# Feed-forward of a streaming encoder layer: two scheduled passes made one product with a written order, and two normalisation factors moved behind the down product

## The chip, the cores and the metric

The kernel runs on one core of one Trainium2 chip. A core has TensorE (PE, matrix products into PSUM, with PEld for its weight loads), VectorE (DVE), ScalarE (ACT), GpSimd (POOL) and SyncE (SP), whose queue issues the transfers. Each engine works off its own queue in order and waits at semaphores for the others. The metric is the device time of one execution in microseconds; the time before is 1810.67 us, the median of three runs (1808.79 to 1811.64).

## The reference

One inference step of a one-layer encoder over 1152 tokens (1024 of a prompt and eight streams of 16): attention beside a gated convolution, cross-attention into a memory, and a gated feed-forward with a causal convolution. Only the last part is touched:

```python
x = x + xo.reshape(b, t_len, D_MODEL) @ w_xo
hf = rms_norm(x, g_ffn)
u_c, new_ffn = causal_dwconv(hf @ w_up, ffn_state, w_ffconv)
x = x + (jax.nn.silu(u_c) * (hf @ w_gate)) @ w_down
...
y_prompt = rms_norm(hp, g_final)
```

The model width is 1024 and the hidden width 2816, that is 8 and 22 blocks of 128. All is float32, and each product of two float32 matrices is made of three passes: both operands are split into a high part and the rest (`h`, `l`), and h·h, h·l and l·h are summed in PSUM. The norm's factor r of a token scales a whole column here (tokens lie along the free axis), so it may be multiplied in before or after a product.

## The kernel before

**Layout.** Activations stand transposed: 128 features in the partitions, 1152 tokens along the free axis. A *split* (`split`, L111 and L112) is a copy on ACT that rounds to the high part (`wh`, `t`, `gx`) and a subtraction on DVE or POOL that gives the rest (`wl`).

**Output projection of the cross-attention** (`residual_wino`). Eight output blocks, each over three token chunks of 384, 24 matmuls a chunk (L148 to L150). When a chunk leaves PSUM, DVE adds the residual (L985, tile `xc`), the sum goes to memory, DVE multiplies by the gain (L987, into `xg`), and ACT and POOL add up the squares. The operand pieces `b` of the next product are split as they come. After the last block stands the norm: a reciprocal over all 1152 tokens (L1005), products with a matrix of ones that sum the squares (L1009), and `rstd` (L190 to L195), whose result is multiplied into the tile `r`.

**Up and gate** (`ffn_up`, `wino`). Two blocks of 128 hidden features at a time form a 2x2 block product in Strassen-Winograd form: seven products P1 to P7 in place of eight, on sums of weights (S1 to S4, POOL, L1030 to L1033) and differences of activations (T1 to T4). A *product* here is 24 matmuls of 288 tokens (L1051). P1 and P2 accumulate in PSUM chain a, P6, P7 and P4 in chain b, P5 and P3 in chain c; between them ACT (L1065, L1072) and DVE (L1061) read the chains into the output tiles `u` (up) or `g` (gate). One call for `u` and one for `g` make a *pair* of 14 products, and there are 11 pairs. In `ffn_conv` (between the two calls) POOL multiplies `u` by r (L1088), ACT and DVE run the three-tap convolution (L1100 to L1104) and ACT the silu (L1105); POOL multiplies its result by r a second time (L1106), for the gate's half, which has not had its r. DVE multiplies with `g` (L1138), and the product goes to the scratch `gscr`.

**Down** (`ffn_down`). For token blocks of 512, 384 and 256 and eight output blocks j: 22 k-tiles times 3 matmuls. The hidden operands are loaded from `gscr` and split into `gx` while j is 0, the weights are loaded and split again for each token block, with the rests on DVE and POOL in turn. `norm` applies the last normalisation, one block late.

**What sets the order.** A scheduler orders each engine's instructions by priorities and modelled times, and places a transfer, a wait or a product of the next stage where it finds room; buffers are counted per pool (three PSUM chains `ch`, three weight buffers, two raw ones).

Of the kernel before, what the change touches and what calls it, by code (L numbers as in the profile page):

```python
# [11 lines left out]
F32R = mybir.dt.float32r  # L12
AF = mybir.ActivationFunctionType
# [38 lines left out]
class Step:  # L52
# [42 lines left out]
    def sm(self, cols):  # L95

        return self.tile("small", "t8", [8], 32)[:, 0:cols]

    def bank(self, tag):
        return self.tile("psum", tag, [1024 if tag in ("sc", "ch") else 512], 3 if tag == "ch" else 2)  # L100
# [868 lines left out]
    def residual_wino(self, wsrc, xh, xl, xsrc, dst, gi):  # L969
# [3 lines left out]
        xg = [None] * KT  # L973
        acc = self.tile(self.tp, "acc", [T])
        self.B = [{} for _ in range(4)]
        self.Tf = [None] * 4
        for n in range(KT):
            j = n // 2 + 4 * (n % 2)
            xg[j] = self.tile("xg", "xg", [T], KT)

            def evac(c, ps):
                cs = slice(c * CH, (c + 1) * CH)
                x = self.tile(self.tp, "xc", [CH], 3)
# [3 lines left out]
                nc.vector.scalar_tensor_tensor(out=xg[j][:, cs], in0=x, scalar=self.g[:, gi, j:j + 1], in1=self.r[:, cs],  # L987
                                               op0=ALU.mult, op1=ALU.mult)
                self.sumsq(acc[:, cs], x, n == 0, sq=self.tile(self.tp, "sq", [CH], 2))

            self.block(wsrc[j], xh, xl, lambda c: ("mm", "tr")[(c + n) % 2], evac)
            if n % 2 == 0:
                k = n // 2
                self.B[k]["B11"] = self.pair("hl", "b", xg[j][:, 0:HT])
            else:
                a, b = xg[j - 4], xg[j]
                b11, b12, b21, b22 = a[:, 0:HT], a[:, HT:T], b[:, 0:HT], b[:, HT:T]
                self.B[k]["B21"] = self.pair("hl", "b", b21)
                self.B[k]["B22"] = self.pair("hl", "b", b22)
                nc.vector.tensor_tensor(out=b11, in0=b12, in1=b11, op=ALU.subtract)  # L1000
                nc.vector.tensor_tensor(out=b12, in0=b22, in1=b12, op=ALU.subtract)
                nc.vector.tensor_tensor(out=b22, in0=b22, in1=b11, op=ALU.subtract)
                nc.vector.tensor_tensor(out=b21, in0=b21, in1=b22, op=ALU.subtract)
                self.Tf[k] = {"T1": b11, "T2": b22, "T3": b12, "T4": b21}
        nc.vector.reciprocal(out=self.r, in_=self.r)  # L1005
        for c in range(NCH):
            cs = slice(c * CH, (c + 1) * CH)
            ps = self.bank("sc")[:, :CH]
            nc.tensor.matmul(ps, lhsT=self.ones, rhs=acc[:, cs], start=True, stop=True)  # L1009
            y, v = (self.tile(self.tp, "xc", [CH], 3) for _ in range(2))  # L1010
            r = self.tile(self.tp, "sq", [CH], 2)
            self.rstd(r, ps, 1.0 / D, CH, y, v)
            nc.vector.tensor_tensor(out=self.r[:, cs], in0=self.r[:, cs], in1=r, op=ALU.mult)
# [6 lines left out]
    def wino_raw(self, u0, u1):  # L1020
        return self.wraw(u0), self.wraw(u1)

    def wino(self, raws, dst, first=False):

        nc = self.nc
        a11, a12 = raws[0][:, 0:512], raws[0][:, 512:1024]
        a21, a22 = raws[1][:, 0:512], raws[1][:, 512:1024]
        s3, s2, s4 = (self.tile("ws", "S", [512], 3) for _ in range(3))
        tt = nc.gpsimd.tensor_tensor
        tt(out=s3, in0=a11, in1=a21, op=ALU.subtract)  # L1030
        tt(out=a21, in0=a21, in1=a22, op=ALU.add)
        tt(out=s2, in0=a21, in1=a11, op=ALU.subtract)
        tt(out=s4, in0=a12, in1=s2, op=ALU.subtract)  # L1033
        opd = {"P1": (a11, "B11"), "P2": (a12, "B21"), "P3": (s4, "B22"), "P4": (a22, "T4"),
               "P5": (a21, "T1"), "P6": (s2, "T2"), "P7": (s3, "T3")}
        ch = {}

        def product(p, c, start):
            x, b = opd[p]
            h, l = self.tile("weights", "wh", [512], 3, F32R), self.tile("weights", "wl", [512], 3, F32R)  # L1040
            self.split(h, l, x)
# [12 lines left out]
        def bank(c):  # L1054
            return ch[c].rearrange("p (t n) -> p t n", t=2)[:, :, 0:HC]

        def sb(m, t):
            return dst[m][t].rearrange("p (t n) -> p t n", t=2)

        def add(m, t, c, y):  # L1060
            nc.vector.tensor_tensor(out=sb(m, t), in0=bank(c), in1=sb(*y), op=ALU.add)  # L1061

        p1 = 1, 0
        product("P1", "a", True)
        nc.scalar.copy(out=sb(*p1), in_=bank("a"))  # L1065
        if first:
            product("P2", "a", False)
        product("P6", "b", True)
        if not first:
            product("P2", "a", False)  # L1070
        add(0, 1, "b", p1)
        nc.scalar.copy(out=sb(0, 0), in_=bank("a"))  # L1072
        product("P7", "b", False)
        product("P5", "c", True)
        add(1, 1, "b", p1)
        product("P4", "b", False)
        add(1, 1, "c", (1, 1))
        product("P3", "c", False)
        add(1, 0, "b", p1)
        add(0, 1, "c", (0, 1))  # L1080


    def ffn_conv(self, f, u):

        nc, I = self.nc, self.I
        st = self.tile("tu", "sff", [NB, 2], 2)
        nc.sync.dma_start(out=st, in_=I["sff"][f])
        nc.gpsimd.tensor_tensor(out=u[:, HALO:HALO + T], in0=u[:, HALO:HALO + T], in1=self.r, op=ALU.mult)  # L1088
        v = self.tile("tu", "vs", [NB, HALO + TS], 2)
        us = u[:, HALO + S_P:HALO + T].rearrange("p (b t) -> p b t", t=TS)  # L1090
        nc.gpsimd.tensor_copy(out=v[:, :, 0:HALO], in_=st)
        nc.gpsimd.tensor_copy(out=v[:, :, HALO:], in_=us)
        new = self.tile("tu", "nff", [18], 2)
        nc.gpsimd.tensor_copy(out=new[:, 0:2], in_=u[:, S_P:S_P + HALO])
        nc.gpsimd.tensor_copy(out=new[:, 2:18].rearrange("p (b t) -> p b t", t=2), in_=v[:, :, TS:TS + 2])
        nc.sync.dma_start(out=self.O["nff"][f], in_=new)
        s = self.tile("tu", "s", [T], 2)
        w = self.wff[:, f]
        sp, ss = s[:, 0:S_P], s[:, S_P:T].rearrange("p (b t) -> p b t", t=TS)
        nc.scalar.activation(sp, u[:, 0:S_P], AF.Identity, scale=w[:, 0:1])  # L1100
        nc.scalar.activation(ss, v[:, :, 0:TS], AF.Identity, scale=w[:, 0:1])
        for j in (1, 2):
            for o, x in ((sp, u[:, j:j + S_P]), (ss, v[:, :, j:j + TS])):
                nc.vector.scalar_tensor_tensor(out=o, in0=x, scalar=w[:, j:j + 1], in1=o, op0=ALU.mult, op1=ALU.add)  # L1104
        nc.scalar.activation(s, s, AF.Silu)  # L1105
        nc.gpsimd.tensor_tensor(out=s, in0=s, in1=self.r, op=ALU.mult)  # L1106
        return s

    def ffn_up(self):

        nc, I = self.nc, self.I

        def halves(z, o=0):
            return z[:, o:o + HT], z[:, o + HT:o + T]
# [303 lines left out]
```

## Time and profile before

| | |
|---|---|
| time, median of three runs | 1810.67 us |
| profiled execution, own time | 1811.96 us |
| profiled execution, span from first to last instruction | 1810.2 us |
| start of the output projection of the cross-attention | about 799 us |
| its last matmul | about 899 us |
| first product of up and gate starts | 916.0 us |
| first matmul of down starts | 1486.5 us |
| last matmul of down ends | about 1798.6 us |

The span is cut at these points because the change reaches only what lies behind 799 us. Times inside the trace are microseconds from the span's start. A row of the timeline or of the chain of waits begins with start and duration; a row of a table of stretches gives the stretch, its length, the busy time of PE with the number of matmuls, the granted TensorE clock (1.00 is full), and the load of the transfer engines.

### The profile page before, as it was taken

To read this page: it belongs to the slowest core of one execution; us is meant where nothing else is said; L and a number is where in the kernel's file an instruction comes from. 1 tells how busy PE (TensorE), PEld (TensorE's weight loads), DVE (VectorE), ACT (ScalarE), POOL (GpSimd) and SP (SyncE) were. 2 spreads that over 40 slices of the span, in tenths; PEclk is the share of its full clock that TensorE was granted. 3 is DMA by queue.
4 is the path that set the end of the run, shared out by engine and by line. 5 is a ranking of instruction groups with operands and counts; after the bars stand their busy time and mean duration, and the time that the engine had idled before them with its cause. 6 is when DMAs were issued, how large, how long until landed. Compare 5 with 4: busy or idle time off the path is not lost.

```text
span 1810.2 us, 28157 instructions
## 1 busy us (share of the span) xinstructions
PE 1687.9 (93%) x10930; PEld 1587.0 (88%) x10930; DVE 1027.9 (57%) x1553; ACT 678.2 (37%) x1385; POOL 613.3 (34%) x548
## 2 busy tenths in 40 slices
PE   8999989999999999999879999999999979999986
PEld 7999878999899999889869889898999967889985
DVE  7756546777633433666776666656556663254355
ACT  7222443555423422443333333333232334353443
POOL 3322232111113311103444445545445433244343
PEclk8999999999999999999989999999999989999999
DMA  5756876543274424514401222121222238355554
GB/s 190 257 194 222 261 239 163 158 142 99 91 265 139 151 95 181 215 67 132 127 25 62 74 64 65 44 74 62 75 74 63 73 122 277 96 167 186 153 151 141
DMA packets 106517, 246.08 MB, mean 136 GB/s; under 512 B 17424, under 2 KB 56720, under 8 KB 106384
## 3 DMA queue, kind: packets, MB, share of 16 engines
q1 hardware_dynamic: 105312, 242.65, 41.3%
q8 instruction: 86, 1.41, 0.3%
q10 hardware_dynamic: 1072, 1.64, 0.3%
q14 instruction: 47, 0.39, 0.1%
HBM read 186.86 MB, written 57.39 MB: 135 GB/s over the span
## 4 chain that ended last, share of the span: by engine, by line
PE 67%; DVE 8%; POOL 8%; DMA 7%; ACT 5%; issue 4%; SPq 0%; DVEq 0%; POOLq 0%; ACTq 0%
PE ch L1051 16%; PE mm L150 11%; PE mm L148 11%; PE mm L149 11%; PE tr L148 3%; POOL u L1088 3%; PE tr L149 3%; PE tr L150 3%; DMA raw<-in_w_ug 2%; DMA raw<-in_w_dn 2%; DMA graw<-gscr 2%; PE tr L653 2%; DVE wl L112 1%; PE sc L614 1%; ACT wh L111 1%
## 5 line engine op out<-in xcount | busy, mean ns | idle before, releaser
L112 POOL TENSOR_TENSOR wl<-raw,wh 128x512 fp32r<-128x512 f32 x126 | 166.8, 1325 | 620.1 <-ACT wh L111 550.1
L111 ACT CAST wh<-raw 128x512 fp32r<-128x512 f32 x340 | 203.9, 604 | 414.9 <-PE mm L149 174.9
L1051 PE MATMUL ch<-t,wh 128*128 128x288 f32 x1408 | 297.0, 305 | 34.4 <-DVE g L1061 34.3
L112 DVE TENSOR_TENSOR wl<-raw,wh 128x512 fp32r<-128x512 f32 (+1 forms) x214 | 188.9, 883 | 224.8 <-ACT wh L111 220.9
L1051 PEld LDWEIGHTS ch<-t,wh 128*128 128x128 f32 x1408 | 236.8, 197 | 37.1 <-DVE g L1061 36.8
L1051 PE MATMUL ch<-b,wh 128*128 128x288 f32 x1056 | 215.3, 298 | 11.2 <-ACT g L1065 7.6
L1051 PE MATMUL ch<-t,wl 128*128 128x288 f32 x704 | 213.6, 306 | 2.2 <-DVE wl L112 1.7
L150 PE MATMUL mm<-gx,wl 128*128 128x512 f32 (+2 forms) x528 | 180.8, 342 | 16.2 <-POOL wl L112 9.7
L148 PE MATMUL mm<-gx,wh 128*128 128x512 f32 (+2 forms) x528 | 179.3, 340 | 10.7 <-ACT gx L111 8.0
L1051 PEld LDWEIGHTS ch<-b,wh 128*128 128x128 f32 x1056 | 170.4, 189 | 15.1 <-ACT g L1065 10.2
L149 PE MATMUL mm<-gx,wh 128*128 128x512 f32 (+2 forms) x528 | 179.6, 340 | 1.8 <-DVE gx L112 1.1
L148 PE MATMUL mm<-xh,wh 128*128 128x384 f32 x496 | 169.6, 342 | 0.9 <-DVE t L822 0.9
L150 PE MATMUL mm<-xh,wl 128*128 128x384 f32 x496 | 167.9, 339 | 0.0
L149 PE MATMUL mm<-xl,wh 128*128 128x384 f32 x496 | 167.6, 338 | 0.0
L1051 PE MATMUL ch<-b,wl 128*128 128x288 f32 x528 | 156.0, 295 | 0.0
L1051 PEld LDWEIGHTS ch<-t,wl 128*128 128x128 f32 x704 | 138.4, 198 | 5.0 <-DVE wl L112 4.9
L150 PEld LDWEIGHTS mm<-gx,wl 128*128 128x128 f32 x528 | 100.5, 190 | 27.3 <-POOL wl L112 13.3
L148 PEld LDWEIGHTS mm<-gx,wh 128*128 128x128 f32 x528 | 100.6, 191 | 21.9 <-ACT gx L111 10.1
L149 PEld LDWEIGHTS mm<-gx,wh 128*128 128x128 f32 x528 | 100.3, 190 | 13.1 <-DVE gx L112 3.8
L1104 DVE SCALAR_TENSOR_TENSOR s<-u,c,s 128x1024 f32<-128x1024 f32 x44 | 80.3, 1825 | 38.1 <-ACT s L1100 38.1
L111 ACT CAST wh<-S 128x512 fp32r<-128x512 f32 x66 | 41.0, 621 | 159.1 <-PE ch L1051 95.7
L1051 PEld LDWEIGHTS ch<-b,wl 128*128 128x128 f32 x528 | 100.2, 190 | 0.0
(364 smaller groups left out, 3725.4 us busy)
## 6 DMA issues: line engine op xcount, KB each, us to landing
raw<-in_w_dn SPq DMA_DIRECT2D x48, 512.0 KB, 3.6
raw<-in_w_ug SPq DMA_DIRECT2D x44, 512.0 KB, 3.6
gscr<-g SPq DMA_DIRECT2D x22, 576.0 KB, 3.8
raw<-in_w_dn SPq DMA_DIRECT2D x24, 384.0 KB, 3.1
kv<-in_kc SPq DMA_DIRECT2D x16, 512.0 KB, 5.7
kv<-in_vc SPq DMA_DIRECT2D x16, 512.0 KB, 6.3
qd<-qscr SPq DMA_DIRECT2D x64, 128.0 KB, 3.7
kv<-in_km SPq DMA_DIRECT2D x16, 512.0 KB, 6.1
```

The source lines that it names most:

```text
L111: self.nc.scalar.copy(out=h, in_=x)
L112: (eng or self.nc.vector).tensor_tensor(out=l, in0=x, in1=fl(h), op=ALU.subtract)
L148: self.nc.tensor.matmul(out, lhsT=ah, rhs=bh, start=i == 0, stop=False)
L149: self.nc.tensor.matmul(out, lhsT=ah, rhs=bl, start=False, stop=False)
L150: self.nc.tensor.matmul(out, lhsT=al, rhs=bh, start=False, stop=i == n - 1)
L614: nc.tensor.matmul(sc[:, a:b], lhsT=qd[:, m, hl, (i % 2) * P:(i % 2 + 1) * P], rhs=ks[m][:, a:b], start=hl == 0, stop=hl == 1)
L653: nc.tensor.matmul(av[:, qs], lhsT=at[kt // 4][:, kt % 4, qs], rhs=vt[:, kt], start=kt == 0, stop=kt == n - 1)
L1051: nc.tensor.matmul(o, lhsT=w[:, ks], rhs=y[:, ts], start=start and k == 0 and i == 0, stop=k == 3 and i == 2, skip_group_check=True)
L1088: nc.gpsimd.tensor_tensor(out=u[:, HALO:HALO + T], in0=u[:, HALO:HALO + T], in1=self.r, op=ALU.mult)
L1104: nc.vector.scalar_tensor_tensor(out=o, in0=x, scalar=w[:, j:j + 1], in1=o, op0=ALU.mult, op1=ALU.add)
```

## The change

The new method `ffn` stands in place of `wino`, `ffn_conv`, `ffn_up`, `ffn_operand` and `ffn_down`, inside a region in which the five engines take the order in which the code is written. The code walks over *slots*: one slot is one product of up and gate (154 of them, list `seq`), or one *step* of down. In slot n every engine is given the read of the chain of product n-1, the split of the weights of product n+3, what the table `at[n]` holds, and then PE the product n.

- The first unit's products stand in another order (P1, P3, P2, P6, P5, P7, ...), with a fourth PSUM chain; PSUM now has four chains of two banks and no other tiles.
- The norm's factor is no longer made ahead of the first product: the sums of squares are taken behind products 5 and 7 (`ones`), and `ratio` computes the new r from r and the sums with Ln and Exp, in place of the reciprocal and `rstd`.
- `u` is multiplied by r on DVE in halves of 576 tokens (`rho`). The second multiplication of the silu by r is gone: DVE multiplies the down product by r when it leaves PSUM (`evac`), 24 times, ahead of the residual.
- Down begins by k-tiles: 22 steps, each with one hidden operand and the weights of four output blocks (12 matmuls of 512 tokens); then by output blocks, steps of four k-tiles. Of the last pair's work, silu, gate and store stand in the first steps of down. Operands of the next token block are loaded singly, three in flight, and split while j is 6 and 7. All weight rests are on DVE.
- The weight pools are new: four buffers each for raw, high and rest. Staging tiles `xc` of the output projection go from three to two, and a chunk that crosses token 576 is written in two pieces.

```diff
-        nc.vector.reciprocal(out=self.r, in_=self.r)
-        for c in range(NCH):
...
-            nc.tensor.matmul(ps, lhsT=self.ones, rhs=acc[:, cs], start=True, stop=True)
...
-        nc.gpsimd.tensor_tensor(out=u[:, HALO:HALO + T], in0=u[:, HALO:HALO + T], in1=self.r, op=ALU.mult)
...
-        nc.gpsimd.tensor_tensor(out=s, in0=s, in1=self.r, op=ALU.mult)
...
+        seq = [(0, "P1"), (0, "P3"), (0, "P2"), (0, "P6"), (0, "P5"), (0, "P7"), (1, "P1"), (0, "P4"),
+               (1, "P2"), (1, "P6"), (1, "P5"), (1, "P7"), (1, "P3"), (1, "P4")]
+        for s in range(2, NFB):
+            seq += [(s, p) for p in ("P1", "P6", "P2", "P7", "P5", "P4", "P3")]
...
+        def rho(i, mt):
+            def f():
+                z = blk(2 * i, mt)
+                nc.vector.tensor_tensor(out=z, in0=z, in1=half(self.r, mt % 10), op=ALU.mult)
+            return f
...
+                nc.scalar.activation(y, r, AF.Square)
+                nc.vector.tensor_scalar(out=two(v), in0=banks(self.rps), scalar1=1.0 / D, scalar2=EPS, op0=ALU.mult, op1=ALU.add)
+                nc.vector.tensor_tensor(out=v, in0=v, in1=y, op=ALU.mult)
+                nc.scalar.activation(y, v, AF.Ln)
+                nc.scalar.activation(y, y, AF.Exp, scale=-0.5)
+                nc.scalar.activation(r, y, AF.Square)
+                nc.vector.scalar_tensor_tensor(out=v, in0=v, scalar=-0.5, in1=r, op0=ALU.mult, op1=ALU.mult)
+                nc.vector.scalar_tensor_tensor(out=r, in0=v, scalar=1.5, in1=y, op0=ALU.add, op1=ALU.mult)
...
+                put(n + 4, rho(i, 0))
+                put(n + 6, rho(i, 11))
+                put(n + 7, rho(i, 10))
+                put(n + 8, rho(i, 1), streams(i, 1), tap0(i, 1))
+                put(n + 9, streams(i, 0), t1[0], tap0(i, 0))
+                put(n + 10, t1[1], t1[2], t1[3])
+                put(n + 11, silu(i, 1), t0[0])
...
+                put(n + 14, silu(i, 0), gate(i, 1, 1))
...
+                put(7, ratio(0))
+                put(8, ratio(1))
+                put(9, rho(0, 0), rho(0, 10))
...
+        steps = [(0, range(4), (k,)) for k in range(NFB)]
+        steps += [(c, (j,), range(4 * u, min(4 * u + 4, NFB)))
+                  for c in range(len(LAST)) for j in range(0 if c else 4, KT) for u in range(6)]
...
+            nc.vector.tensor_tensor(out=t, in0=ch.pop((c, j)), in1=self.r[:, a:b], op=ALU.mult)
+            nc.vector.tensor_tensor(out=x, in0=t, in1=x, op=ALU.add)
...
+        for n in range(N):
+            if n:
+                read(n - 1)
+            if n + 3 < N:
+                split(n + 3)
+            else:
+                wsplit(n + 3 - N)
+            for f in at[n]:
+                f()
...
+            product(n)
+            if n in (5, 7):
+                ones(n == 7)
...
+            if c and js[0] == 1 and ks[0] == 0:
+                norm2(c - 1)
+            step(i)
...
+            if c < 2 and j >= 6:
+                operands(NFB * (c + 1) + (ks[0] // 4 + 1 if j == 6 else min(10 + ks[0], NFB)))
...
+        with self.tc.manual_schedule(engines={E.PE, E.DVE, E.Activation, E.Pool, E.SP}):
+            self.ffn()
```

Three places show what moves. First, DVE's queue from the last chunk of the output projection on. `xc` is the staging tile of the residual, `xg` (after: `xa`, `xb`) the gained activations, `wl` weight rests, `t` and `b` operand rests. Before:

```order
L985 TENSOR_TENSOR xc_9126<-tr_9101,xc_9126 128x384
L112 TENSOR_TENSOR wl_9341<-S_9276,wh_9340 128x512
L987 SCALAR_TENSOR_TENSOR xg_9024<-xc_9126,c_6_79,c_9_84 128x384
L112 TENSOR_TENSOR t_9208<-xg_8316,t_9207 128x576
L1001 TENSOR_TENSOR xg_8910<-xg_9024,xg_8910 128x576
L112 TENSOR_TENSOR b_9139<-xg_9024,b_9138 128x576
L1005 RECIPROCAL c_9_84<-c_9_84 128x1152
L1002 TENSOR_TENSOR xg_9024<-xg_9024,xg_8910 128x576
L191 TENSOR_SCALAR xc_9150<-sc_9147 128x384
```

The same place in the change, where `wl_9190`, `wl_9194` and `wl_9198` are the rests of the first three products P1, P3 and P2, and `S_1663` is the weight sum S4:

```order
L988 TENSOR_TENSOR xc_9140<-tr_9115,xc_9140 128x384
L993 SCALAR_TENSOR_TENSOR xa_8922<-xc_9140,c_6_79,c_9_84 128x384
L112 TENSOR_TENSOR b_9153<-xa_8922,b_9152 128x576
L112 TENSOR_TENSOR wl_9190<-raw_9174,wh_9189 128x512
L112 TENSOR_TENSOR wl_9194<-S_1663_9183,wh_9193 128x512
L112 TENSOR_TENSOR wl_9198<-raw_9174,wh_9197 128x512
L1007 TENSOR_TENSOR xa_8922<-xb_8923,xa_8922 128x576
L1007 TENSOR_TENSOR xb_8923<-xa_8922,xb_8923 128x576
L1007 TENSOR_TENSOR xa_8922<-xa_8922 128x576
L112 TENSOR_TENSOR wl_9205<-S_1662_9181,wh_9204 128x512
L112 TENSOR_TENSOR t_9213<-xa_8211,t_9212 128x576
```

The reciprocal and `rstd` have left this place; behind the last chunk stands the rest of P1, then one that waits for the fourth weight sum, and the differences behind it. On SP, the second weight load of the first unit (`raw_9176`), from which these sums are made, now stands behind the last store of `xc`:

```order
L1030 DMA raw_9174<-in_w_ug 128x1024
L989 DMA x_4_76<-xc_9140 128x384
L1030 DMA raw_9176<-in_w_ug 128x1024
L1030 DMA raw_9208<-in_w_ug 128x1024
L1030 DMA raw_9210<-in_w_ug 128x1024
```

Second, POOL's queue over one pair in the middle of up and gate (`S` and `raw` weight sums, `vs` and `nff` the streams' states). Before:

```order
L1033 TENSOR_TENSOR S_10498<-raw_10235,S_10497 128x512
L1088 TENSOR_TENSOR u_10232<-u_10232,c_9_84 128x1152
L1092 COPY vs_10474<-u_10232 128x8x16
L1088 TENSOR_TENSOR u_10231<-u_10231,c_9_84 128x1152
L1092 COPY vs_10455<-u_10231 128x8x16
L1094 COPY nff_10458<-u_10231 128x2
L1094 COPY nff_10477<-u_10232 128x2
L1095 COPY nff_10477<-vs_10474 128x16
L1095 COPY nff_10458<-vs_10455 128x16
L1123 MEMSET u_10713 128x2
L1091 COPY vs_10937<-sff_10934 128x8x2
L1106 TENSOR_TENSOR s_10462<-s_10462,c_9_84 128x1152
```

and in the change:

```order
L1045 TENSOR_TENSOR S_1800_10057<-raw_9884,raw_9886 128x512
L1131 COPY vs_10089<-sff_9981 128x8x2
L1132 COPY vs_10089<-u_9779 128x8x16
L1134 COPY nff_10092<-u_9779 128x2
L1135 COPY nff_10092<-vs_10089 128x16
L1045 TENSOR_TENSOR raw_9886<-raw_9886 128x512
L1045 TENSOR_TENSOR S_1811_10137<-raw_9886,raw_9884 128x512
L1045 TENSOR_TENSOR S_1819_10232<-raw_9884,S_1811_10137 128x512
```

The four multiplications of 1152 elements a pair have left POOL; the sums are spread between the slots. Third, SP's queue where the operands of the second token block are loaded (`graw`, after: `S`). Before:

```order
L116 DMA raw_14895<-in_w_dn 128x1024
L1146 DMA graw_15548<-gscr_77 128x2x384
L1146 DMA graw_15558<-gscr_77 128x2x384
L1146 DMA graw_15568<-gscr_77 128x2x384
L116 DMA raw_14905<-in_w_dn 128x1024
L1146 DMA graw_15578<-gscr_77 128x2x384
L1146 DMA graw_15588<-gscr_77 128x2x384
```

and in the change, from the first step of j = 7 on:

```order
L1030 DMA raw_15532<-in_w_dn 128x768
L1314 DMA S_2541_15551<-gscr_77 128x384
L1314 DMA S_2544_15557<-gscr_77 128x384
L1314 DMA S_2547_15563<-gscr_77 128x384
L1314 DMA S_2550_15569<-gscr_77 128x384
L1314 DMA S_2555_15591<-gscr_77 128x384
L1314 DMA S_2558_15597<-gscr_77 128x384
L1314 DMA S_2561_15603<-gscr_77 128x384
L1314 DMA S_2564_15609<-gscr_77 128x384
L1030 DMA raw_15615<-in_w_dn 128x1024
```

An operand is now one load of one k-tile where it was half of a load of two, and sixteen of them stand in the four steps of j = 7.

More of the change, by code (lines that the diff above doesn't have):

```diff
@@ L1018, in pair, with w2 @@
         return h, l
[L1020 to L1041, printed above, removed]
+    def w2(self, x, view=lambda z: z):
+        m = x.shape[-1] if len(x.shape) == 2 else 512
+        h, l = (self.tile("w2", t, [512], 4, F32R)[:, 0:m] for t in ("wh", "wl"))
+        self.split(view(h), view(l), x)
+        return h, l
@@ L1052, in product @@
                                          stop=k == 3 and i == 2, skip_group_check=True)
[L1054 to L1107, printed above, removed]
@@ new lines, in read @@
+        def read(n):
+            s, p = seq[n]
+            for c, o, y in (first if s == 0 else second if s == 1 else reads)[p]:
+                if y is None:
+                    nc.scalar.copy(out=two(blk(s, o)), in_=banks(ch[s, c]))
+                else:
+                    nc.vector.tensor_tensor(out=two(blk(s, o)), in0=banks(ch[s, c]), in1=two(blk(s, y)), op=ALU.add)
+        def rho(i, mt):
[3 more added lines that the diff above has]
+            return f
@@ new lines, in load, with sums, f, reopen @@
+        def load(s):
+            return lambda: self.ffn_load(s)
+        def sums(s, *ds):
+            def f():
+                for d in ds:
+                    self.ffn_sum(s, d)
+            return f
+        def reopen():
+            self.close("xa")
+            self.open("tu", "right")
+        put(0, load(1), tsplit("T2", range(4)))
+        put(1, tsplit("T1", (0, 1)))
+        put(2, tsplit("T1", (2, 3)), reopen)
+        put(3, tsplit("T3", (0, 1), (1,)))
+        put(4, tsplit("T3", (2, 3), (3,)), self.tsubs[3])
@@ new lines, in qsplit, with operands @@
+        def qsplit(q):
+            x = graw.pop(q)
+            e = q % 28
+            pool, tag, bufs = ("tb", "t", 24) if e < 12 else ("t8", "gx", 8) if e < 16 else ("hl", "b", 24)
+            h, l = (self.tile(pool, tag, [512 if pool == "t8" else HT], bufs, F32R)[:, 0:x.shape[-1]] for _ in range(2))
+            self.split(h, l, x, nc.gpsimd if q % 3 == 0 else None)
+            gx[divmod(q, NFB)] = h, l
+        def operands(upto):
+            while done[0] < min(upto, 3 * NFB):
+                q = done[0]
+                qsplit(q)
+                if q + 3 < 3 * NFB:
+                    qload(q + 3)
+                done[0] += 1
```

410 lines of the change are left out of this document (294 added, 116 removed).

## The prediction

> **What bounds the kernel now.** I read the page's busy times and its chain first, then PE alone over the stretches that the change reaches, then who PE waits for there. The page:
>
> ```profile
> PE 1687.9 (93%) x10930; PEld 1587.0 (88%) x10930; DVE 1027.9 (57%) x1553; ACT 678.2 (37%) x1385; POOL 613.3 (34%) x548
> PE 67%; DVE 8%; POOL 8%; DMA 7%; ACT 5%; issue 4%; SPq 0%; DVEq 0%; POOLq 0%; ACTq 0%
> ```
>
> PE is busy 93% of the span, but a third of the chain that ended last lies on others. Where PE stands still shows in the table of stretches (stretch, length, PE's busy time and matmuls, granted clock, the transfers' share and GB/s):
>
> ```profile
> 898.90:916.00 17.10, 3.05 (x7) 0.61 0.16 42
> 916.00:970.10 54.10, 47.27 (x311) 0.90 0.11 31
> 970.10:1479.60 509.50, 470.81 (x3387) 0.97 0.21 66
> 1063.30:1103.20 39.90, 39.42 (x297) 1.00 0.25 84
> ...
> 1486.50:1798.60 312.10, 290.39 (x1589) 0.99 0.55 170
> 1545.00:1600.00 55.00, 55.00 (x245) 1.00 0.33 99
> 1655.00:1705.00 50.00, 50.00 (x285) 0.98 0.54 164
> 1740.00:1747.00 7.00, 7.00 (x60) 1.00 0.53 142
> 1798.60:1810.20 11.60, 1.74 (x9) 0.73 0.47 160
> ```
>
> The fourth row is a stretch in which PE is fed: 39.90 / 297 = 0.1343 us a matmul of 288 tokens, so a pair (14 products of 24) would take 336 x 0.1343 = **45.1 us**. The third row holds ten pairs: 50.95 us each, 5.85 too many. In down, fed stretches give 55.00 / 245 = 0.2245, 50.00 / 285 = 0.1754 and 7.00 / 60 = 0.1167 us a matmul for 512, 384 and 256 tokens; with 528 of each that is 118.5 + 92.6 + 61.6 = **272.7 us**, against 312.1 taken. From 899 us on PE needs 496 + 273 us of 911; about 140 us are waits, half clock and the end. The waits:
>
> ```profile
> PE ch L1051 <- DVE g L1061: 34.3, 11, 3.2
> PE sc L1009 <- DVE xc L191: 11.8, 1, 11.8
> PE mm L150 <- POOL wl L112: 9.7, 12, 2.7
> PE mm L148 <- ACT gx L111: 8.0, 3, 6.9
> PE ch L1051 <- ACT g L1065: 7.6, 11, 1.0
> PE mm L150 <- DVE wl L112: 6.2, 4, 2.6
> ```
>
> Eleven times, once a pair, PE waits 3.1 us for a read of chain b by DVE, and eleven times 0.7 for ACT. Why DVE is late there (rows of POOL, DVE and PE in one pair):
>
> ```profile
> 1105.36 2.67 POOL L1106 TENSOR_TENSOR s<-s,c 128x1152 f32<-128x1152 f32 x1
> ...
> 1105.45 3.67 DVE L1104 SCALAR_TENSOR_TENSOR s<-u,c,s 128x1024 f32<-128x1024 f32 x1
> ...
> 1109.31 0.74 DVE L1061 TENSOR_TENSOR g<-ch,g 128x576 f32<-128x576 f32 x1
> ...
> 1110.11 0.52 PE L1051 MATMUL ch<-t,wh 128*128 128x288 f32 x2 [3.15 <-DVE g L1061]
> ```
>
> All four taps of the second block stand in DVE's queue ahead of the read, and one lasts 3.67 us because POOL's multiplication by r runs at its side; PE goes on right behind the read. Of the 5.85 us a pair, 3.1 + 0.7 are this wait and ACT's; the other 2.0 are matmuls at a lower granted clock behind it (0.97 in the third row, 1.00 in the fed one).
>
> **Up and gate after the change.** These rows price its instructions; with three times in a row, the middle one is the median and the first the least; the last three give, behind the bar, busy time and the mean of one in ns:
>
> ```profile
> L112 DVE TENSOR_TENSOR wl<-raw,wh x79: 674/692/2664, 959.6 to 1451.7; 128x512 fp32r<-128x512 f32 x79
> L1030 POOL TENSOR_TENSOR S<-raw,raw x20: 1286/1295/1447, 965.8 to 1443.3; 128x512 f32<-128x512 f32 x20
> DMA to landing us min/median/max: 3.4/3.6/6.3
> L1104 DVE SCALAR_TENSOR_TENSOR s<-u,c,s x32: 1279/1284/3680, 1001.0 to 1358.6; 128x1024 f32<-128x1024 f32 x32
> L1104 DVE SCALAR_TENSOR_TENSOR s<-vs,c,s x32: 337/347/352, 1002.2 to 1362.2; 128x128 f32<-128x128 f32 x32
> L1106 POOL TENSOR_TENSOR s<-s,c 128x1152 f32<-128x1152 f32 x20 | 57.8, 2891 | 16.7 <-ACT s L1105 16.4
> L1088 POOL TENSOR_TENSOR u<-u,c 128x1152 f32<-128x1152 f32 x20 | 50.8, 2540 | 0.0
> L111 ACT CAST wh<-raw 128x512 fp32r<-128x512 f32 x340 | 203.9, 604 | 414.9 <-PE mm L149 174.9
> ```
>
> POOL loses (57.8 + 50.8) / 10 = 10.9 us a pair, both multiplications by r. DVE takes over the first in four halves; a half of 576 is nearest to the subtraction of that size, 0.74 (below). DVE's work for a pair is 14 weight rests x 0.69 + 10 chain reads x 0.74 + 4 halves of r x 0.74 + taps 4 x 1.28 + 4 x 0.35 + 4 gate halves x 0.74 = 9.7 + 7.4 + 3.0 + 6.5 + 3.0 = **29.6 us of 45.1**. POOL keeps 8 sums x 1.3 = 10.4 and some 3 of small copies; if all of that stopped DVE, DVE would have 43, still under 45.1. What matters is the slot of 3.22 us: the read of product n-1 has until product n+1, one slot. The fullest slots (9, 11, 12 of a pair) give DVE 0.74 + 0.69 + 1.28 = 2.7; with one POOL sum in the way 4.0, and the overrun of 0.8 is inside the 3.22 - 0.74 = 2.5 us that a read may be late. Weight rests are three slots ahead. So I cost the eight added instructions at nothing, covered by DVE's idle third, and put ten pairs at 10 x 45.1 = **451 us** (509.5 before). If the cover is gone, see the first rival. The 0.7 us behind ACT goes too: P1's chain is read with P6 and P2's read is waited for by nobody soon.
>
> A rule speaks against this. The Trainium skill, "TensorE: Matmul & The Clock Gate", section "A second HAM failure mode: psum-queue depth-cycling", says that a kernel that changes PSUM banks from group to group can idle a little so often that its clock keeps falling and rising. The fed row disagrees so far: 1.00 over 39.90 us with chains a, b and c in turn.
>
> **The start.** Rows around 900 us, and the four sums of a unit in POOL's queue with the load ahead of them:
>
> ```profile
> 900.22 0.61 DVE L987 SCALAR_TENSOR_TENSOR xg<-xc,c,c 128x384 f32<-128x384 f32 x1
> ...
> 902.23 0.74 DVE L1001 TENSOR_TENSOR xg<-xg,xg 128x576 f32<-128x576 f32 x1
> 902.90 0.75 DVE L112 TENSOR_TENSOR b<-xg,b 128x576 fp32r<-128x576 f32 x1
> 903.57 7.34 DVE L1005 RECIPROCAL c<-c 128x1152 f32<-128x1152 f32 x1
> ```
> ```profile
> 1033.98 3.60 DMA raw<-in_w_ug
> 1037.81 1.30 POOL S L1030
> ...
> 1042.25 1.30 POOL S L1033
> ```
>
> The 17.1 us between the last product of the projection (899.0) and the first of up go: reciprocal, ones and `rstd` (11.8 waited at L1009). What is late next: P1's high weights stand on ACT behind the last operand's copy: addition, gain, copy, copy are four steps of 0.6 to 0.7, and with 0.4 for hand-overs it starts at about 899.0 + 3.0. P3, second, needs all four sums of weights, whose second load now stands behind the last store: issue 1.3 us after 899.0, then 9.6 us from issue to the last sum (1033.98 to 1043.55), and a copy: 11.4 after 899.0. P1 ends at 8.0 if it runs at a lower clock, so PE waits **3.4**. Behind it on DVE's queue stand the other rests, three differences and T2: 0.7 + 2.2 + 0.7 + 4 x 0.75 = 6.6 us, done 18.6 after 899.0, and P6, which reads T2, comes at 19.8. `ratio` is new: four steps of 0.75 on DVE around three of ACT (0.60 for 512, so 0.7 each), twice, in slots 7 and 8; DVE falls some 5 us behind, and P7 waits about **1.3** for P6's read. Two stretches at lower clock cost 2 x 2.0 by the pair above, the four products with ones, 0.2 to 0.3 each by the last row of the table of stretches, 1.2. The first pair ends at 899.0 + 3.0 + 45.1 + 3.4 + 1.3 + 4.0 + 1.2 = 899.0 + **58.0** (71.1 before). Bounds: 46 with no wait, 71 if the new waits are as long as the old.
>
> **Down.** The 6.9 us at its start (waits, fourth row) go: the first operands and weights are split in the last slots of up; 0.5 stays. In steps of 2.7, 2.1 and 1.4 us DVE has one weight rest of 0.7, so POOL's slow ones (9.7 us of waits) are not missed, and the multiplication by r on leaving PSUM, 24 x some 0.5 (0.74 for 576) = 12 us on DVE, lies beside PE. What comes instead is the refill: sixteen operands of the next block are taken in the last four steps, three in flight.
>
> ```profile
> xc<-x SPq DMA_DIRECT2D x24, 192.0 KB, 2.4
> x<-xc SPq DMA_DIRECT2D x24, 192.0 KB, 2.6
> graw<-gscr SPq DMA_DIRECT2D x11, 384.0 KB, 4.4
> ```
>
> A load of 192 KB takes between 2.4 (first row) and 4.4 (third, twice the size), with its split 3.6 to 5.6; the weights for the first step of the new block stand behind the twelfth operand, those of the second behind the sixteenth. Nine loads are three rounds, thirteen 4.3: 12 to 18 and 17 to 26 us from the first of these steps, when PE has work for 12. That is 5 to 11 us for each of the two changes of block; I take 7 and 8, nearer to the row of the same size. Add 3 for lower clock behind them, 2 for the last norm in DVE's queue (six multiplications and `rstd`'s seven steps, each some 0.5, stand in front of weights that are four steps of 1.4 ahead) and 2 for the ones: 272.7 + 15 + 7 = **294.7** (312.1 before). Bounds: 279 with hardly a wait, 312 with no gain.
>
> Two `xc` tiles instead of three: store, load and addition are 2.6 + 2.4 + 0.6 = 5.6 us of the 8.4 between two uses (48 matmuls of 0.1754); nothing, or up to 10 us if the transfers took over 1.5 times as long. The eight split writes are on a DVE that has room there. The end: one more DVE step of 0.4, a smaller last store; 11.6 as before.
>
> **The sum**, against the profiled execution (span 1810.2, own time 1811.96): 899.0 + 58.0 + 451 + 0.5 + 294.7 + 11.6 = 1714.8 of span, and 1.8 around it: **1717 us**. The profiled execution is 0.07% above the median, which changes nothing here. About 0.2% is what a measurement of this kernel can tell from no change.
>
> **Rivals.**
> - *DVE becomes the bound of up and gate.* For: 29.6 + 13 of POOL's, and every wait of its queue for ACT, come near 45. Against: DVE's rests are three slots ahead. At 48.5 a pair, 10 x 3.4 more: 1751. Chance 0.15.
> - *Down keeps its pace*, the refill being as long as its upper end and the last norm later: 312 in place of 295: 1734. Chance 0.17.
> - *PE's clock falls at changes of chain.* One stretch of 2.0 us a pair, as behind the waits now: 20 more, 1737. Chance 0.05; the page named above would have it so.
> - *Hardly a wait is left*: start 3, refill 4: 1717 - 12 - 14 = 1691. Chance 0.13.
> - *Slower.* In a fixed order one late instruction holds all behind it: if reads of chains stand behind taps that wait for ACT, PE waits in most products. The gain is 95 us, so this decides from 95 / 154 = 0.62 us a product on; now PE waits 0.27 a product. Nothing in the slots' sums says so: at 0.75 a product 1717 + 154 x 0.75 = 1832. Chance 0.03.
>
> The forecast has 0.47. The range takes in the first three rivals and stops at the fourth: **1692 to 1756**. Faster 0.96, within 0.2% 0.01, slower 0.03.
>
> **What would show it.** A table of stretches with pairs of 45 to 46 us at clock 1.00, and POOL's rows of 1152 gone; one wait of 3 to 4 us of PE for ACT's copy of S behind P1; waits of PE for `wh` or `wl` at the two changes of token block, 5 to 11 us each, and few elsewhere in down; the same 899 at the end of the projection. I am wrong if waits of PE for reads of chains come once a pair again, if the projection ends later than 902, or if down is over 312.

## The result, and the profile after

The changed kernel takes 1734.84 us (median of four runs, 1733.6 to 1735.65) where the kernel before, run beside it, takes 1810.53: a ratio of 0.9582, 95% interval 0.9566 to 0.9599. The prediction was 1717 with a range of 1692 to 1756. Its profiled execution has a span of 1733.8 us. The page, first busy times, then the chain of work that ended last:

```profile
PE 1669.3 (96%) x10930; PEld 1579.6 (91%) x10930; DVE 1045.0 (60%) x1707; ACT 678.1 (39%) x1382; POOL 413.9 (24%) x443
PE 80%; DVE 6%; DMA 5%; ACT 4%; issue 2%; POOL 1%; SPq 0%; DVEq 0%; ACTq 0%; POOLq 0%
```

POOL has lost 200 us of work, and PE's share of the chain has risen from 67% to 80%. Stretches of PE, with columns as before the change: the first pair with its start, ten pairs, down, the end, and then short ones in which the clock is to be seen:

```profile
893.00:957.50 64.50, 54.35 (x340) 0.87 0.19 62
957.50:1405.60 448.10, 448.10 (x3367) 1.00 0.23 78
...
1405.60:1722.90 317.30, 292.71 (x1590) 0.95 0.55 170
1722.90:1733.80 10.90, 1.52 (x6) 0.80 0.29 96
...
897.00:899.00 2.00, 2.00 (x10) 0.50 1.00 393
...
905.00:907.00 2.00, 2.00 (x10) 0.50 0.18 33
...
947.00:949.00 2.00, 2.00 (x11) 0.50 0.03 8
...
1534.00:1536.00 2.00, 1.90 (x6) 0.50 0.36 97
...
1644.00:1654.00 10.00, 8.56 (x35) 0.50 0.28 79
```

Ten pairs run without a gap at full clock, 44.8 us each. From the end of the projection to the end of up and gate it is 512.6 us (1405.6 - 893.0), 580.6 before (1479.6 - 899.0): 68 of the 76 us gained. Down is as long as it was: 317.3 against 319.0 with its old start (1798.6 - 1479.6). PE's waits in the first pair, and from down to the end of its work (waited for, us in total, times, longest):

```profile
PE ch L1102 <- ACT wh L111: 5.5, 2, 2.9
PE ch L1102 <- DVE xb L1111: 3.7, 1, 3.7
```
```profile
PE ch L1381 <- ACT wh L111: 21.3, 10, 6.3
PE ch L1381 <- DVE wl L112: 2.7, 5, 1.3
```

In down PE now waits for the weights' copies by ACT. Two places make most of it. The first is a change of token block; rows of ACT, and the one of PE behind them:

```profile
1527.73 1.00 ACT L111 CAST t<-S 128x384 fp32r<-128x384 f32 x2 [1.88 <-DMA S<-gscr]
...
1532.44 0.51 ACT L111 CAST t<-S 128x384 fp32r<-128x384 f32 x1 [3.72 <-DMA S<-gscr]
1532.86 0.61 ACT L111 CAST wh<-raw 128x512 fp32r<-128x512 f32 x1
...
1533.53 0.69 PE L1381 MATMUL ch<-b,wh 128*128 128x384 f32 x1 [6.32 <-ACT wh L111]
```

The copy of the weights that PE waits for stands behind an operand's copy (`t<-S`), which waits 3.72 us for its load. That operand is not used until two steps later. The second place is the last norm of the block that is done:

```profile
1556.08 5.87 DVE L1364 TENSOR_TENSOR ys<-ys,nt 128x512 f32<-128x512 f32 x6
1556.12 3.47 POOL L1364 TENSOR_TENSOR ys<-ys,nt 128x512 f32<-128x512 f32 x2 [12.50 <-DVE nt L195]
...
1557.95 2.01 ACTq L1365 DMA_DIRECT2D out_yT<-ys  x2
...
1560.06 1.97 ACT L111 CAST wh<-raw 128x512 fp32r<-128x512 f32 x4 [5.46 <-DMA out_yT<-ys]
1560.73 0.62 PE L1381 MATMUL ch<-t,wh 128*128 128x384 f32 x2 [2.09 <-ACT wh L111]
```

Two of the eight outputs are multiplied on POOL and stored from ACT's queue; ACT stands for 5.46 us until POOL is done, and behind it are four copies of weights.

### The profile page after: what moved, and what is told of

Read it like the earlier page. It is cut to its first block, busy times and chain, and to the rows that moved or that the text cites. A ratio compares the mean times of both kernels' runs of the same rounds, so it can differ in the third digit from the quotient of the medians.

```text
span 1733.8 us, 28155 instructions
## 1 busy us (share of the span) xinstructions
PE 1669.3 (96%) x10930; PEld 1579.6 (91%) x10930; DVE 1045.0 (60%) x1707; ACT 678.1 (39%) x1382; POOL 413.9 (24%) x443
## 4 chain that ended last, share of the span: by engine, by line
PE 80%; DVE 6%; DMA 5%; ACT 4%; issue 2%; POOL 1%; SPq 0%; DVEq 0%; ACTq 0%; POOLq 0%
PE ch L1102 27%; PE ch L1381 11%; PE mm L148 8%; PE mm L150 8%; PE mm L149 8%; PE tr L148 3%; PE tr L149 3%; PE tr L150 3%; DMA S<-gscr 2%; PE tr L653 2%; DMA ys<-x 1%; PE sc L614 1%; PE tr L640 1%; ACT wh L111 1%; DVE ys L1364 1%
## 5 line engine op out<-in xcount | busy, mean ns | idle before, releaser
L1102 PE MATMUL ch<-t,wh 128*128 128x288 f32 x1408 | 284.9, 297 | 3.9 <-DVE xb L1111 3.7
L1102 PEld LDWEIGHTS ch<-t,wh 128*128 128x128 f32 x1408 | 227.5, 189 | 4.6 <-issue 3.9
L112 POOL TENSOR_TENSOR wl<-raw,wh 128x512 fp32r<-128x512 f32 x54 | 71.5, 1326 | 450.8 <-ACT wh L111 412.6
L1381 PE MATMUL ch<-t,wh 128*128 128x512 f32 (+2 forms) x544 | 139.5, 343 | 6.5 <-ACT wh L111 6.3
L1381 PEld LDWEIGHTS ch<-t,wh 128*128 128x128 f32 x544 | 97.0, 192 | 15.4 <-ACT wh L111 7.9
L1381 PE MATMUL ch<-b,wh 128*128 128x256 f32 (+2 forms) x384 | 95.8, 341 | 13.0 <-ACT wh L111 13.0
L1381 PE MATMUL ch<-t,wl 128*128 128x512 f32 (+2 forms) x272 | 94.0, 346 | 2.8 <-DVE wl L112 2.5
L148 PEld LDWEIGHTS mm<-xh,wh 128*128 128x128 f32 x496 | 93.3, 188 | 3.7 <-issue 1.6
L149 PEld LDWEIGHTS mm<-xl,wh 128*128 128x128 f32 x496 | 93.4, 188 | 0.4
L150 PEld LDWEIGHTS mm<-xh,wl 128*128 128x128 f32 x496 | 93.4, 188 | 0.1
L1045 POOL TENSOR_TENSOR S<-raw,raw 128x512 f32<-128x512 f32 x44 | 72.1, 1640 | 68.1 <-DVE wl L112 63.6
```

Of the source, the lines that this page charges most:

```text
L112: (eng or self.nc.vector).tensor_tensor(out=l, in0=x, in1=fl(h), op=ALU.subtract)
L148: self.nc.tensor.matmul(out, lhsT=ah, rhs=bh, start=i == 0, stop=False)
L149: self.nc.tensor.matmul(out, lhsT=ah, rhs=bl, start=False, stop=False)
L150: self.nc.tensor.matmul(out, lhsT=al, rhs=bh, start=False, stop=i == n - 1)
L1045: self.nc.gpsimd.tensor_tensor(out=w[o], in0=w[x], in1=w[y], op=op)
L1102: nc.tensor.matmul(o, lhsT=w[:, ks], rhs=y[:, ts], start=start and k == 0 and i == 0, stop=k == 3 and i == 2, skip_group_check=True)
```

## The experiments

Four are on up and gate, six on down, one on the start, and one profiles the kernel before once more.

### Why up and gate are faster

Two explanations stood against each other: the written order, which keeps reads of chains ahead of blocks of taps, and POOL, which no longer multiplies at DVE's side. The first experiment spoils the order alone:

```diff
-                put(n + 9, streams(i, 0), t1[0], tap0(i, 0))
-                put(n + 10, t1[1], t1[2], t1[3])
-                put(n + 11, silu(i, 1), t0[0])
-                put(n + 12, t0[2])
-                put(n + 13, t0[1], t0[3])
+                put(n + 9, streams(i, 0), tap0(i, 0))
+                put(n + 11, *t1)
+                put(n + 12, silu(i, 1), *t0)
...
+            late = n >= 14 and n % 14 in (11, 12)
+            if n and not late:
                 read(n - 1)
...
             for f in at[n]:
                 f()
+            if late:
+                read(n - 1)
```

> The changed kernel, with the four taps of each block of ten pairs put back into one slot each (slots 11 and 12 of a pair) and the read of that slot behind them. Theory 'order' (up and gate gain because a read never stands behind a whole block of taps): DVE needs 0.69 + 2 x 1.28 + 2 x 0.35 + 0.74 = 4.7 us before the read is done in a slot of 3.2, so PE waits about 1.5 us twice a pair, 3.0 x 10 = 30 us: 1765 us, with two PE waits of 1 to 2 us for a read of chain b or c in each pair. Rival 'POOL' (the old wait was POOL's 1152-wide multiplication at DVE's side, which stays away here): at most the 0.8 us a pair that was left of the old 3.15 without the stretched tap: 1735 to 1743 us.

1765.53 us, ratio to before 0.9753 [0.9736, 0.9769]. PE's waits over the ten pairs:

```profile
PE ch L1102 <- DVE xb L1111: 23.7, 17, 1.8
```

In this written order the place of the taps is worth 31 us, as reckoned from the durations on DVE's queue. The second gives work back to POOL:

```diff
-                nc.vector.tensor_tensor(out=z, in0=z, in1=half(self.r, mt % 10), op=ALU.mult)
+                nc.gpsimd.tensor_tensor(out=z, in0=z, in1=half(self.r, mt % 10), op=ALU.mult)
```

> The changed kernel, with the four half-width multiplications of u by r of a pair given back to POOL (4 x some 1.27 us by half of the old 2.54). Theory 'order': POOL's work may stretch a tap or a read of DVE by about 1.3 us, less than the 2.5 us that a read may be late, so pairs stay at 44.8 to 45.3 us: 1735 to 1740 us. Rival 'POOL': a wait of about 3 us a pair comes back: 1760 to 1770 us.

1733.38 us, 0.9577 [0.9563, 0.9591]: no difference from the changed kernel that could be measured, and the view of PE's waits from 957 us to the end of up is empty. POOL's row for this line (least, median and longest in ns):

```profile
L1116 POOL TENSOR_TENSOR u<-u,c x44: 1204/1582/1818, 938.4 to 1381.4; 128x576 f32<-128x576 f32 x44
```

So 44 multiplications of 1.58 us on POOL are harmless here. The other two take the multiplications out of the old kernel, whose order is the scheduler's; the factor r is then missing from its outputs, and only its time is of use:

```diff
-        nc.gpsimd.tensor_tensor(out=u[:, HALO:HALO + T], in0=u[:, HALO:HALO + T], in1=self.r, op=ALU.mult)
...
-        nc.gpsimd.tensor_tensor(out=s, in0=s, in1=self.r, op=ALU.mult)
```

> The kernel before without its two multiplications by r on POOL in up and gate (the norm factor is left out of u and of s); everything else and its order as before. Theory 'order': the block of taps still stands ahead of the read; the stretched tap falls from 3.67 to 1.28, so the wait of 3.15 a pair falls to about 0.8 and its lower clock with it: 11 x 2.4 = 26, with clock up to 45 us less than 1810: 1765 to 1784 us. Rival 'POOL': both the wait and the lower clock go, 11 x 5.85 = 64 us: about 1746 us. If the projection ends near 899 us in this profile too, the 6 us by which it ends earlier after the change belong to the change; if it ends near 893, they do not.

> The kernel before without the second of its two multiplications by r on POOL alone (s times r, behind the gate's silu; that factor is left out of the output). Theory 'one' (the wait once a pair is that multiplication beside DVE's taps, the first one stands where DVE has time): nearly the whole gain of leaving both out, 1743 to 1752 us. Rival 'each its share' (POOL's busy time counts, whichever it is): about half of the 67 us: 1770 to 1780 us. Rival 'order' (the block of taps ahead of the read): 1800 us or more.

With both out: 1742.98 us, 0.963 [0.9616, 0.9645]. With the second alone out: 1769.16 us, 0.9778 [0.9761, 0.9795]. Up and gate in the two, as one stretch each:

```profile
908.70:1406.40 497.70, 495.30 (x3696) 0.99 0.23 71
```
```profile
911.40:1434.70 523.30, 504.52 (x3696) 0.99 0.21 68
```

Before it was 563.6 (916.0 to 1479.6) for eleven pairs: 51.2 us a pair, 47.6 without the second multiplication, 45.2 without both. The theory of the order, 1765 to 1784, misses the first of these by 22 us, and the second lies next to "each its share". Taking out the second multiplication gains 3.6 us a pair in the old order, and the first, taken out after it, 2.4; without them that order has hardly a wait left, and is 0.4 us a pair behind the new one. In the second run these waits stay, 0.7 us each once a pair:

```profile
PE ch L1051 <- DVE g L1061: 8.0, 11, 0.8
PE ch L1051 <- ACT g L1065: 7.9, 11, 1.0
```

The two multiplications cost time in two ways. The second stretches a tap: without it none of the 40 long taps of DVE takes over 1.29 us, where the longest was 3.68 before. The first makes the taps late: ACT's first tap waits for it, and DVE stands in front of its own taps, ahead of the read, for ACT. The first long tap of a pair on DVE, with the second multiplication out and with both out:

```profile
1085.73 1.28 DVE L1104 SCALAR_TENSOR_TENSOR s<-u,c,s 128x1024 f32<-128x1024 f32 x1 [3.55 <-ACT s L1100]
```
```profile
1072.80 1.28 DVE L1103 SCALAR_TENSOR_TENSOR s<-u,c,s 128x1024 f32<-128x1024 f32 x1 [0.63 <-ACT s L1099]
```

So leaving out these two multiplications gives the old kernel nearly all that the change gives up and gate. The first one costs 2.4 us a pair in the old order and, in halves, nothing in the new; whether the halves or the places make it harmless was not taken apart, and the second was not put back on POOL in the new order.

### Why down is not

Refill first. The first edit (two operands a step in place of four) keeps three staging buffers, the second has five (and ten `ys` tiles in place of eleven, to make room):

```diff
-                operands(NFB * (c + 1) + (ks[0] // 4 + 1 if j == 6 else min(10 + ks[0], NFB)))
+                operands(NFB * (c + 1) + (u + 1 if j == 6 else 8 + 2 * u))
+            elif c and j == 0:
+                operands(NFB * c + min(20 + 2 * u, NFB))
```

> The changed kernel, with the refill of operands at a change of token block spread: two operands a step through the last j and the first two steps of the new block, in place of four a step. Theory 'queue' (PE waits for weights because their copy stands in ACT's queue behind up to eight operand copies that each wait for a load; the loads themselves would be in time): the waits of 7.5 and 8.4 us at the two changes go, and 8 to 10 us of half clock behind them: 1709 to 1719 us. Rival 'transfers' (the loads of the new block cannot land earlier, whatever the order): PE waits for operands in place of weights: 1730 to 1737 us.

```diff
-            graw[q] = self.tile("ws", ("S2", "S3", "S4")[q % 3], [512])[:, 0:b - a]
+            m = q % 3 if q < NFB else (1, 2, 0, 3, 3)[(q - NFB) % 5]
+            graw[q] = (self.tile("ws", ("S2", "S3", "S4")[m], [512]) if m < 3 else self.tile("t8", "gr", [384], 2))[:, 0:b - a]
...
-                if q + 3 < 3 * NFB:
-                    qload(q + 3)
+                for z in (q + 3,) if q < NFB - 1 else range(q + 3, q + 6) if q == NFB - 1 else (q + 5,):
+                    if z < 3 * NFB:
+                        qload(z)
```

> The changed kernel, with five staging buffers for the refill of operands in place of three, and all else in its order (ten ys tiles in place of eleven make the room). Theory 'three in flight' (an operand takes some 4.2 us from the issue of its load to its split, so three buffers give one per 1.45 us, and the 16 of the last j take 23 us where PE has 16 us of work): with five, one per 0.85 us and 14 us, so the waits for weights at the first change of block go, at the second 2 us stay, and the half clock behind them goes: 16 - 2 + 7 = 21 us less than 1735: 1710 to 1719 us. Rival 'transfers' (the 16 loads and the weights share what the DMA engines give): the waits of 7.5 and 8.4 us stay: 1732 to 1737 us.

1728.3 us, 0.9549 [0.9535, 0.9564], and 1719.21 us, 0.9505 [0.9491, 0.9519]. The first gain, 6.5 us, lies between the two expectations; the second, 15.6, ends 0.2 us above the upper edge of what "three in flight" gave. The kernel before took 1807.8 to 1810.3 us (medians) beside the runs of this section, so a difference of 2 or 3 us between two of them says little. Waits for the weights' copies in down, the slower refill and the five buffers:

```profile
PE ch L1381 <- ACT wh L111: 17.3, 6, 4.3
```
```profile
PE ch L1383 <- ACT wh L111: 11.4, 6, 3.1
```

The transfers are not the limit: with five in flight one takes 3.2 to 3.3 us in place of 2.9 (medians of the loads of 192 KB from 1505 to 1545 us), and from ACT's first copy of an operand in the last j to its twelfth it is 9.9 us in place of 17.6. The norm is spread over eight steps:

```diff
-            for j in (0, 6, 1, 2, 7, 3, 4, 5):
-                eng, q = (nc.vector, nc.sync) if j < 6 else (nc.gpsimd, nc.scalar)
+            def out(j):
+                eng, q = (nc.vector, nc.sync) if j < 6 or c < 2 else (nc.gpsimd, nc.scalar)
...
+                outs.extend((out, j) for j in range(KT))
...
+            elif outs:
+                f, z = outs.pop(0)
+                f(z)
```

> The changed kernel, with the last norm of the first two token blocks spread: one multiplication by the factor and one store in each of the eight steps behind it, all on DVE and on SP's queue, in place of six multiplications in a row on DVE and two on POOL with their stores in ACT's queue. Theory 'queue' (ACT stands 4 to 5 us in front of the weights' copies because its two stores wait for POOL): the waits of 2.1 + 1.3 and 3.1 + 0.8 us behind the norms go and some 5 us of half clock with them: 1721 to 1727 us. Rival 'transfers' (the eight stores and the loads of weights meet at the DMA engines, near a share of 1.0 there): the waits stay: 1732 to 1738 us.

1726.21 us, 0.9547 [0.9531, 0.9563]: 8.6 us less. The next fills four of PE's waits with matmuls that serve nothing:

```diff
+W0 = (10, 10, 24, 18)
...
+        def warm(z, m):
+            for _ in range(m):
+                nc.tensor.matmul(z[:, 0:P], lhsT=self.ones, rhs=self.ones, start=True, stop=True, skip_group_check=True)
...
+                if n < 2:
+                    warm(ch[c], W0[n])
...
+                    elif c and j == 0:
+                        warm(z, W0[1 + c])
```

> The changed kernel, with multiplications of the constant ones by themselves, into a bank that the next product starts anew, ahead of the first two products of up (10 and 10) and of the first step of the second and third token block (24 and 18), about 0.22 us each: PE is then busy through most of four waits. Theory 'idle clock' (PE runs at 0.50 for 4 to 10 us because it stood still for 2.5 us or more before): the stretches at 0.50 behind these waits go, worth about 2, 3, 3 and 4 us, of which the first is given back to the wait for S4: 1724 to 1729 us. Rival (the clock falls for another reason, as a change of chain or of load): the clock in the rows stays at 0.50 behind these places and the added work costs a little: 1734 to 1738 us.

1735.88 us, 0.9591 [0.9576, 0.9606]: the same as without them. Stretches of PE at the first change of block (added matmuls, then the first steps of the new block) and over all of down:

```profile
1525.70:1531.00 5.30, 5.30 (x49) 1.00 0.79 274
...
1531.00:1536.00 5.00, 2.57 (x12) 1.00 0.37 105
```
```profile
1404.20:1722.90 318.70, 299.35 (x1674) 0.97 0.54 170
```

The theory of the idle clock is right on the clock here, which stays at 1.00 where it was 0.50 (1534 to 1536 above), and wrong on the time. PE does its steps faster and then waits for the next weights: at 1534 us for another 2.2. Down takes 318.7 us in place of 317.3. At the start, the other place with added matmuls, up and gate end 1.4 us earlier (1404.2 in place of 1405.6), where about 3 were forecast. The waits behind the norms were not filled. Last, the edits together:

> Five staging buffers and the spread norm together. If the two causes lie apart, as theory 'queue' for the norm and 'three in flight' for the refill have it, the gains add: 1735 - 15.6 - 8.6 = 1710 to 1713 us. If both are one limit of the transfers, the better of the two remains: 1717 to 1720 us.

> Five staging buffers, the spread norm and two operands a step in place of four. With five in flight an operand comes every 0.85 us, two in 1.7 us of steps of 2.7 and 2.1, so the last waits for weights at the two changes (2.2 and 3.8 us with five buffers) and their half clock go: 1702 to 1708 us, down at 285 to 290 us. Rival 'transfers': as without the spreading, 1710 to 1713 us.

1713.62 us, 0.9474 [0.9449, 0.9498], and 1706.87 us, 0.9431 [0.9409, 0.9453]. Buffers and norm gain 21.2 of the 24.2 us that they gain singly, so 1713.62 lies 0.6 us above the 1710 to 1713 of two separate causes and 3.4 below the 1717 of one limit. The third edit adds 6.7 us where the rival gave nothing. Down, in the last, 0.1 us above the 290 expected:

```profile
1405.80:1695.90 290.10, 281.50 (x1590) 0.99 0.59 186
```

This version beats both kernels, the changed one by 28 us.

### The start, and the kernel before once more

On top of this version the order of the first products is changed, and `ratio` is cut into `f`, up to ACT's last square, and `g`, DVE's last two steps:

```diff
-        seq = [(0, "P1"), (0, "P3"), (0, "P2"), (0, "P6"),
+        seq = [(0, "P1"), (0, "P2"), (0, "P3"), (0, "P6"),
...
-                put(7, ratio(0))
-                put(8, ratio(1))
-                put(9, rho(0, 0), rho(0, 10))
+                (f0, g0), (f1, g1) = ratio(0), ratio(1)
+                put(7, f0)
+                put(8, g0, f1)
+                put(9, rho(0, 0), rho(0, 10), g1)
```

> The same with the first pair in another order: product P2 second and P3 third, so that S4 has one product's time more, and the two halves of the norm factor's work cut so that DVE goes on with reads while ACT works on them. The wait for S4 (2.9 us) becomes one of about 1 us for ACT's read of P1, the wait of 3.7 us for a read of chain b goes, and with them 3 to 5 us of half clock: 7 to 11 us less than the kernel without these two edits: 1693 to 1700 us. If the clock takes as long to come back whatever the wait, 4 to 5 us less.

1709.92 us, 0.9449 [0.9429, 0.9469], not better than the 1706.87 without these two edits, and 9.9 us over the upper end that was expected. PE's longest wait and the rows of ACT that make it:

```profile
PE ch L1102 <- ACT u L1109: 6.7, 1, 6.7
```
```profile
902.52 1.14 ACT L111 CAST wh<-S 128x512 fp32r<-128x512 f32 x2 [7.08 <-POOL u L1177]
...
906.73 0.64 ACT L1109 COPY u<-ch 128x576 f32<-128x576 f32 x1
```

ACT's read of P1, for which P2 waits, stands behind the copies of S and of operands that ACT already had in its queue; moving the product without them made a wait of 2.9 into one of 6.7. The wait for the read of chain b also grew, from 3.7 to 5.3 us.

> The kernel before, profiled once more. In its first profile the projection ended at 898.9 us, in all others of this study, two with the same instructions up to there, between 889.8 and 893.6. Theory 'the program': this profile shows 898 to 900 again, and the 6 us belong to the kernel before as it is placed. Theory 'the execution': it shows 890 to 894 and the span is 4 to 8 us shorter than 1810 or the time is lost elsewhere.

It ran in 1810.92 us, with a span of 1809.1. The end of the projection, the start, up and gate, down and the tail:

```profile
880.00:890.70 10.70, 10.70 (x63) 1.00 0.35 115
890.70:908.30 17.60, 3.11 (x8) 0.69 0.16 41
908.30:1473.60 565.30, 519.76 (x3696) 0.96 0.20 63
1473.60:1796.40 322.80, 291.99 (x1588) 0.98 0.56 172
1796.40:1809.10 12.70, 2.91 (x10) 0.63 0.41 138
```

The projection ends 8 us earlier than in the first profile of the same kernel, and the later stages take 7 us longer. So the 6 us by which it ends earlier after the change are not the change's, and a stage of one profile is known to a few us only.

## Why the prediction was right, and where it was not

**Up and gate: right.** Ten pairs were put at 451 us and took 448.1; POOL's multiplication stretches a tap, the read stands behind it, and with both multiplications gone the wait is gone. The runs without them show it in the old kernel itself. The prediction named the second one alone; what the first costs by making the taps late it did not see, though the change takes away both. The eight added instructions of DVE cost nothing, as costed. The rival in which DVE is the bound (48.5 us a pair) did not come about. Where the taps were stacked a pair took 48.0 (480.1 / 10), but by reads that stand behind taps, which is the mechanism of the rival "slower".

**The clock at changes of chain: right.** The rule weighed there, in the Trainium skill's "TensorE: Matmul & The Clock Gate", section "A second HAM failure mode: psum-queue depth-cycling", does not show here: four chains change all the time, PE has no idle time between them, and the clock is 1.00 over 448.1 us.

**The first pair: its place right, its size 6.5 us short.** 58.0 was forecast and 64.5 came. Start 2.5 (3.0 forecast) and the wait for S4 2.9 (3.4) hold. The wait at P7 for the work of `ratio` was 3.7 in place of 1.3. The lower clock was put at 4.0: it is 0.50 behind all three waits, for 17.1 us in all, and takes some 8 us (54.35 busy against 45.1 + 1.2).

**Down: wrong, 317.3 in place of 294.7**, over the 312 from which the prediction called itself wrong. The step that failed is its sum of small terms over 272.7: 15 for the refill, 3 for lower clock, 2 for the last norm, 2 for the ones. They are 22 together, and 44.6 came.

- *The refill.* The mechanism was right: three loads in flight set the rate, and PE waits for weights whose copy stands behind the operands'. 7 and 8 us were put at the two changes of block, and the gaps of PE there sum to 7.6 and 8.4. That this came so near is in part luck: j = 7 has six steps, of which the first four take the sixteen operands, so PE's work before the change is 66 x 0.2245 = 14.8 us at the first one and not 12 (66 x 0.1754 = 11.6 at the second), while the twelfth operand came after 17.6 us, late in the 12 to 18 that were reckoned. Mending the refill gains 15.6 us by buffers and 6.7 more by its pace, some 22 in place of 18 with its clock.
- *The norm.* It was put at 2, as work of some 0.5 us an operation in DVE's queue. The six multiplications on DVE took 5.87 us at the first norm in place of some 3, and there are waits of 3.4 and 3.9 us behind the two norms, most of them ACT's wait for POOL in a queue that the prediction did not look at. Spread, it gains 5.6 to 8.6 us (with and without five buffers).
- *The lower clock.* It was put at 3. PE was busy for some 23 us of down at 0.50, which is 11 us by pace alone. But at the two changes of block the added matmuls show that this is no price of its own: with most of it gone there and the refill as it was, down stays as long.
- *The rest.* With rate and norm mended down takes 290.1 us, still 17.4 over 272.7 where only the 2 for the ones were left. In that run the blocks of 384 and 256 tokens start at 1526.48 and 1619.02 us, so the three blocks take 120.7, 92.5 and 76.9 us against 118.5, 92.6 and 61.6: 15 us lie in the block of 256 tokens, whose steps are the shortest, and PE stands still for 8.2 of them. Another 2 are a floor put too low: the stretch of 7 us was too short to read 0.1167 from, the rows of 256 tokens stand 0.120 us apart (3 in 0.36). What would mend the last block was not tried.

**The sum.** The first pair's 6.5 and down's 22.6 us too many stand against 6.0 from the projection, 2.9 from the pairs and 1.2 from boundary and tail: 19.0 us more span than forecast. The 6.0 are not the change's, as the second profile of the kernel before shows, so the total came nearer than its terms deserved. The rival "down keeps its pace" gave 1734, with the refill and the norm as its causes, and that is what happened; that its number is met so closely is luck, since down took 317.3 where it had 312, the first pair was longer too, and the 6.0 made up for it.

## What to carry to other kernels

A wait is named after the instruction that came last, but in a written order the cause is often what stands ahead of it in that engine's queue: list the queue between two uses of the late engine, with each thing that it waits for, before pricing a step. An operation of POOL can cost time at two places, by stretching one of DVE's at its side (3.67 us in place of 1.28) and by making late what waits for it (some 3 us ahead of the taps), and it is worth asking whether algebra can move it to where a tile is touched anyway. Where a chain of loads, copies and splits set the pace, as at the changes of block, making PE faster only moved its waits; more loads in flight, asked for at the pace at which they come, shortened them.

## What the runs showed of the hardware

The granted clock is 1.00 or 0.50 in nearly every short stretch where PE works. Read in stretches of 0.2 us, the time at 0.50 comes in pieces of 3.41 us and whole multiples of it: after the change 3.41 from 896.6 us, 6.82 from 903.4, 944.4, 1531.4 and 1668.0, 3.41 from 1562.2, and 13.66 from 1640.6, where several waits follow one another. A piece can begin after PE has gone on: PE started at 895.50 behind its wait of 2.53 us, and the clock fell at 896.6. The length of a wait does not settle it alone. In the kernel before, the wait for chain b (2.8 to 3.2 us) comes once in each of eleven pairs and the clock fell behind nine of them; with the stacked taps, a wait of 1.8 us comes once in each of ten pairs and it fell at three. Behind the others it stayed at 1.00, as here, in a stretch right behind one:

```profile
1143.00:1147.00 4.00, 3.41 (x24) 1.00 0.00 0
```

The Trainium skill, "TensorE: Matmul & The Clock Gate", section "Part 1: The HAM clock gate", gives the same two states and one idle window of some 3.4 us for the fall; here 2.53 us were enough at 893 us.
